# Two mixer stages of a hybrid backbone: priorities from the longest chain of data dependences instead of hand-written offsets

## The chip, the cores and the metric

One core of a Trainium2 chip runs the kernel. The metric is device time in microseconds (us), the median over runs of the whole program. The engines are PE (TensorE, matmul), DVE (VectorE), ACT (ScalarE), POOL (GpSimd) and SP (SyncE); SP, ACT and POOL also issue DMA transfers, each in the order of its own queue.

## What is computed

A backbone of two layers on 512 latent tokens (stream `l`) and 256 context tokens (stream `c`), D = 1024. Cut to what matters, each layer is

```
h        = rms_norm(x, g1) * (1 + scale1) + shift1       # modulated by the condition vector
u        = h @ W_in                                      # columns for four head groups of 256 channels
y        = concat(ssd(u), hyena(u), retention(u), s5(u)) # the mixers; latent tokens read the
                                                         # final context states of the recurrent ones
x        = x + gate1 * (y @ W_out)
f        = rms_norm(x, g2) * (1 + scale2) + shift2
x        = x + gate2 * ((silu(f @ W_g) * (f @ W_u)) @ W_d)
```

SSD is a chunked scan in both directions, Hyena a pair of long convolutions done as matrix products with cosine and sine tables (its filters come from a small MLP with sines), retention a chunked linear attention with rotations, S5 a diagonal complex state space model done in blocks. The second layer has no output for the context tokens.

## The kernel before

Everything is one program of some 15,000 instructions. A weight piece of 128 x 1024 floats is loaded into a staging tile `wst` (three buffers in a ring, issued on SP, L207), then split in two parts that TensorE takes at full precision together: `whi` by a copy on ACT (L155) and `wlo` by a subtraction on DVE (L134). The normed stream is split likewise (`ahl`/`alol` for the latent tokens, `ahc`/`aloc` for the context). A projection is three products a tile: `whi*ah`, `whi*al`, `wlo*ah` (`mm3`, called by `proj`, L233). All matmuls stand on line L126 in the profile, since one helper issues them; so the tiles' names tell them apart.

PSUM banks come from four rings: `mm` 3 banks, `xa` 2, `xb` 2, `md` 1. A "flow" of work takes banks from its own ring. `ps_mm` mostly holds products of the input projection, `ps_xb` those of Hyena and its filters, `ps_xa` those of SSD, retention and S5. The one bank `ps_md` holds in turn the modulation (`mod`, L334: 16 products `wst,csil` of a weight piece and the condition vector, ACT copies the row to `mrow`, PE turns it by a product with `const`, DVE adds the bias into `modv`) and the blocks of S5 (`s5k`, `KT`, `gt`).

What sets the order: each traced instruction carries a priority number, and a scheduler that walks through the program takes at each step, of the instructions whose inputs are there by its own estimate, the one with the lowest number. So each engine gets one fixed order, and at run time it waits in that order. Before, the numbers are counters that `body` (L1572) starts by hand:

- `at(p)` (L114) lets the instructions of a block count from p on; `flow(fl, p)` does so and sets the ring; `bulk()` (L240) adds 300000, so that the products of `proj` come after the mixers' own.
- `in_proj` (L1031) gives the q-th block of 256 columns the number PB + 4000q, and the modulation that is computed beside it PB + 2000q + 1000.
- The mixers start at `chunk(q)` = PB + 50000 + 2000q + 1000, with q chosen per mixer and layer: `chunk(2)` for Hyena of the context, `chunk((5, 0)[i])` for Hyena of the latent tokens, `chunk((-20, -5)[i])` for the output of S5, `chunk((4, 2)[i])` for SSD, and so on.
- In layer 0 the S5 tables (50000), the start (10000), the filters (35000 to 45000) and the S5 matrices (40000) have their own numbers.

The stages in order of time: start and norm of layer 0 (0 to about 90 us), layer 0's projection with filters, modulation, S5 blocks and mixers (to about 600 us), output projection and feed-forward, then layer 1's projection and mixers (about 1200 to 1585 us), and its feed-forward.

Of the kernel before, what the change touches and what calls it, by code (L numbers as in the profile page):

```python
# [9 lines left out]
F32 = mybir.dt.float32  # L10
# [8 lines left out]
L = 512  # L19
# [14 lines left out]
def halves(a):  # L34
    """A table as two float32 parts that float32r carries exactly."""
# [71 lines left out]
class Kern:  # L107
# [6 lines left out]
    @contextmanager  # L114
    def at(self, p):
        """Instructions in this block get priorities from p on."""
        tc = self.tc
        old, tc.cur_priority = tc.cur_priority, p
        try:
            yield  # L120
        finally:
            tc.cur_priority = old

# [37 lines left out]
    def pst(self):  # L161
        """A PSUM bank from the ring of the current flow of work."""
# [5 lines left out]
    def pst2(self, fl="mm+xb"):  # L168
        """As pst, from two rings in turn where no mixer runs."""
# [6 lines left out]
    def flow(self, fl, p=None):  # L176
        """Work that takes its banks and small tiles from rings of its own; p: its priority."""
# [10 lines left out]
    def rsq(self, v, n):  # L188
        """v: (128, n) tile, replaced by 1/sqrt(v)."""
# [13 lines left out]
    def piece(self, src, nk, ncol):  # L203
        """src: (128, nk * ncol) of a weight laid out by pieces."""
# [5 lines left out]
    def weights(self, srcs, nk=8):  # L210
        """Pieces of 128 columns as high and low parts."""
# [7 lines left out]
    def held(self, src):  # L219
        """Four tiles of rows of a weight with all its columns, src: (8, 128, 512)."""  # L220
# [20 lines left out]
    def bulk(self):  # L241
        """Products that fill the tensor engine come after the mixers' own."""
# [34 lines left out]
    def put_y(self, s, k, t, c0=0):  # L277
        """Keep tile k of the mixers' output: as operands of the output projection where these have room already."""
# [12 lines left out]
    def ytiles(self, s, p):  # L291
        """Tiles that are not written in the order of their making: each has its own place."""
# [41 lines left out]
    def mod(self, i, c0, c1):  # L334
        """Columns 256*c0 .. 256*c1 of the modulation of layer i."""
# [15 lines left out]
    def mod_vec(self, i, cols, both, p):  # L351
        """As mod for tiles of columns, with a column of the weights a row: products and sums on VectorE.
        The context stream has the tiles in both only."""
# [16 lines left out]
    def gains(self, i, part, s, gat):  # L370
        """(1 + scale) * g for a stream; part is 1 or 4."""
# [4 lines left out]
    def sq_acc(self, s, x, acc, first):  # L376
        """acc += x*x"""
# [7 lines left out]
    def rinv_rows(self, s, accs, scale, c0=0, c1=None):  # L385
        """Per-token 1/sqrt(scale * sum over channels + eps), broadcast to all partitions in PSUM."""
# [14 lines left out]
    def segs(self, s):  # L401
        """Ranges of tokens that are normed one after the other, so that products of one hide the norm of the next."""
# [1500 lines left out]
```

## Time and profile before

| | before |
|---|---|
| median of 3 runs | 1915.59 us (1913.96 to 1918.56) |
| span of the profiled execution | 1919.5 us |
| PE busy in it | 1790.1 us (93%) |
| DVE, ACT, POOL busy | 1257.5, 713.5, 207.3 us |
| moved by DMA | 280.87 MB, mean 146 GB/s |

For the profiled execution no time is given beside its span; the span lies 3.9 us above the median and 0.9 us above the longest of the runs shown. In the tables of the profile, "out<-in" names the tile written and the tiles read, "<-" behind a wait names what ended it, and PEclk is the TensorE clock that was granted as a share of full speed.

### The profile page before, as it was taken

To read this page: it belongs to the slowest core of one execution; us is meant where nothing else is said; L and a number is where in the kernel's file an instruction comes from. 1 tells how busy PE (TensorE), PEld (TensorE's weight loads), DVE (VectorE), ACT (ScalarE), POOL (GpSimd) and SP (SyncE) were. 2 spreads that over 40 slices of the span, in tenths; PEclk is the share of its full clock that TensorE was granted. 3 is DMA by queue.
4 is the path that set the end of the run, shared out by engine and by line. 5 is a ranking of instruction groups with operands and counts; after the bars stand their busy time and mean duration, and the time that the engine had idled before them with its cause. 6 is when DMAs were issued, how large, how long until landed. Compare 5 with 4: busy or idle time off the path is not lost.

```text
span 1919.5 us, 28992 instructions
## 1 busy us (share of the span) xinstructions
PE 1790.1 (93%) x10792; PEld 1526.3 (80%) x10792; DVE 1257.5 (66%) x2941; ACT 713.5 (37%) x1390; POOL 207.3 (11%) x273
## 2 busy tenths in 40 slices
PE   3789878898999999999999999989999999999997
PEld 2678767686789888888888989878866888888886
DVE  8788764778858899777665427678576843233336
ACT  4354234555227223212132115514673542222222
POOL 0201121123002000011223000121110000000000
PEclk9899979998899999999999999999997999999998
DMA  6656588765612335656635513565563322222331
GB/s 231 178 138 186 149 180 229 243 192 160 203 56 89 121 123 164 219 190 230 210 113 131 155 44 123 158 207 159 153 201 96 126 73 94 89 96 88 97 101 56
DMA packets 193089, 280.87 MB, mean 146 GB/s; under 512 B 51745, under 2 KB 127837, under 8 KB 192436
## 3 DMA queue, kind: packets, MB, share of 16 engines
q1 hardware_dynamic: 107188, 166.20, 28.5%
q10 hardware_dynamic: 55920, 64.72, 10.9%
q0 software_dynamic: 29840, 48.09, 8.9%
q8 instruction: 85, 1.39, 0.3%
q14 instruction: 56, 0.46, 0.1%
HBM read 235.00 MB, written 43.96 MB: 145 GB/s over the span
## 4 chain that ended last, share of the span: by engine, by line
PE 58%; DVE 11%; issue 8%; DMA 8%; ACT 3%; POOL 1%; ACTq 0%; SPq 0%; DVEq 0%; POOLq 0%
PE ps_mm L126 31%; PE ps_xb L126 20%; PE ps_xa L126 4%; DMA mvw<-in_wmt_dram 4%; PE ps_md L126 2%; DMA wst<-in_wi_dram 1%; ACT L155 1%; DVE mvo L364 1%; DVE wlo L134 1%; DVE gt L134 1%; DVE t L134 1%; DVE g L1499 1%; DVE cst L134 1%; DVE s5tmp L134 1%; ACT whi L155 1%
## 5 line engine op out<-in xcount | busy, mean ns | idle before, releaser
L155 ACT ACTIVATE whi<-wst 128x1024 fp32r<-128x1024 f32 (+3 forms) x226 | 198.9, 917 | 361.5 <-PE ps_mm L126 169.4
L134 DVE TENSOR_TENSOR wlo<-wst,whi 128x1024 fp32r<-128x1024 f32 (+3 forms) x226 | 233.9, 1058 | 83.5 <-ACT whi L155 81.2
L126 PE MATMUL ps_mm<-alol,whi 128*128 128x512 f32 (+1 forms) x688 | 262.7, 383 | 0.4 <-POOL alol L134 0.4
L126 PE MATMUL ps_mm<-ahl,wlo 128*128 128x512 f32 (+1 forms) x688 | 262.3, 382 | 0.0
L126 PE MATMUL ps_mm<-ahl,whi 128*128 128x512 f32 (+1 forms) x688 | 260.9, 383 | 0.3 <-ACT ahl L155 0.2
L126 PE MATMUL ps_mm<-h,whi 128*128 128x512 f32 (+1 forms) x592 | 168.8, 365 | 0.9 <-DVE h L134 0.7
L126 PE MATMUL ps_xb<-ahl,whi 128*128 128x512 f32 (+1 forms) x416 | 154.2, 373 | 3.8 <-ACT ahl L155 3.8
L126 PE MATMUL ps_xb<-ahl,wlo 128*128 128x512 f32 (+1 forms) x416 | 153.8, 370 | 0.0
L126 PE MATMUL ps_xb<-alol,whi 128*128 128x512 f32 (+1 forms) x416 | 153.5, 371 | 0.1
L134 DVE TENSOR_TENSOR sg<-sg,ps_mm 128x512 f32<-128x512 f32 (+1 forms) x70 | 39.9, 570 | 172.9 <-PE ps_mm L126 172.7
L126 PEld LDWEIGHTS ps_mm<-alol,whi 128*128 128x128 f32 x688 | 130.7, 190 | 26.4 <-issue 2.7
L126 PEld LDWEIGHTS ps_mm<-ahl,wlo 128*128 128x128 f32 x688 | 130.7, 190 | 24.5 <-issue 1.1
L126 PEld LDWEIGHTS ps_mm<-ahl,whi 128*128 128x128 f32 x688 | 130.2, 191 | 25.0 <-issue 1.6
L126 PE MATMUL ps_xb<-h,whi 128*128 128x256 f32 (+1 forms) x592 | 129.2, 310 | 0.1
L364 DVE SCALAR_TENSOR_TENSOR mvo<-mvw,crow 128x1024 f32<-128x1024 f32 x80 | 97.8, 1222 | 39.6 <-DMA mvw<-in_wmt_dram 38.7
L126 PE MATMUL ps_mm<-ahc,whi 128*128 128x256 f32 x368 | 107.4, 296 | 13.0 <-ACT whi L155 8.6
L126 PEld LDWEIGHTS ps_mm<-h,whi 128*128 128x128 f32 x592 | 103.7, 188 | 17.5 <-DVE h L134 1.2
L126 PE MATMUL ps_mm<-aloc,whi 128*128 128x256 f32 x368 | 108.2, 295 | 1.0 <-DVE aloc L134 1.0
L126 PE MATMUL ps_mm<-ahc,wlo 128*128 128x256 f32 x368 | 107.1, 293 | 2.0 <-DVE wlo L134 2.0
L126 PEld LDWEIGHTS ps_xb<-h,whi 128*128 128x128 f32 x592 | 98.9, 188 | 11.6 <-issue 1.1
L126 PE MATMUL ps_mm<-h,wlo 128*128 128x512 f32 (+1 forms) x296 | 107.9, 365 | 0.0
L155 ACT ACTIVATE h<-sg 128x512 fp32r<-128x512 f32 (+1 forms) x70 | 37.4, 534 | 161.7 <-DVE sg L134 161.6
(576 smaller groups left out, 4137.3 us busy)
## 6 DMA issues: line engine op xcount, KB each, us to landing
wst<-in_wu_dram SPq DMA_DIRECT2D x88, 512.0 KB
mvw<-in_wmt_dram POOLq DMA_DIRECT2D x56, 512.0 KB, 3.7
wst<-in_wi_dram SPq DMA_DIRECT2D x42, 512.0 KB
wst<-in_wm_dram SPq DMA_DIRECT2D x40, 512.0 KB
wst<-in_wd_dram SPq DMA_DIRECT2D x24, 384.0 KB
ftab<-in_c_ftL_dram POOLq DMA_DIRECT2D x32, 256.0 KB, 5.0
wst<-in_wd_dram SPq DMA_DIRECT2D x32, 256.0 KB
s5rot<-s5r SPq DMA_DIRECT2D x32, 192.0 KB
```

What stands on the lines that cost most here:

```text
L126: return self.nc.tensor.matmul(out, lhsT, rhs, start=start, stop=stop)
L134: return (eng or self.nc.vector).tensor_tensor(out, a, b, op=op)
L155: return self.nc.scalar.activation(out, in_, func, bias=bias, scale=scale)
L364: self.nc.vector.scalar_tensor_tensor(o, st, 1.0, crow[:, q], op0=ALU.mult, op1=ALU.mult, accum_out=mv[:, c, q:q + 1])
L1499: nc.vector.tensor_tensor_scan(o, dcy, x, 0.0, ALU.mult, ALU.add)
```

## The change

The program is traced twice. From the first trace, `priorities` computes for each instruction the length of the longest chain of data dependences from it to the end, with a length for each instruction from `length` (a table of costs by engine and size that the change writes down itself). Edges that only say that a buffer is free again are not followed. All matmuls into one PSUM tile share the rank of the first. In two ranges of the old numbers, 0 to 1500000 (all of layer 0 up to its output projection) and 2000000 to 2500000 (layer 1's projection and mixers), the instructions are sorted anew: first those that are not `bulk`, within each class those with the longer chain first, and numbered through. In layer 0 a product counts as `bulk` only from 1350000 on, so those that the start issues early do not. The second trace gives each instruction its new number. The norm of layer 1, both output projections and both feed-forwards keep the old numbers. What each instruction computes, its tiles and its engine stay; the rest of the diff takes out comments.

```diff
+class Ranked(tile.TileContext):
+    ranks = None
+    def instruction_hook(self, ins):
+        if not self.ranks:
+            return super().instruction_hook(ins)
+        keep = self.cur_priority
+        self.cur_priority = self.ranks.pop(0)
+        super().instruction_hook(ins)
+        self.cur_priority = keep + 1
+
+MIXED = ((0, 1500000), (2000000, 2500000))
...
+def length(i):
+    out = getattr(i.outs[0], "bass_ap", None) if i.outs else None
...
+    n = elements(out)
...
+    if kind == "InstDMACopy":
+        return 2500 + n * 128 // 50
+    if i.engine == mybir.EngineType.PE:
+        return max(112, 0.46 * n) if i.ins[0].dtype == F32R else 2 * max(112, 0.85 * n)
+    if i.engine == mybir.EngineType.Activation:
+        return 300 + 0.83 * n
+    if i.engine == mybir.EngineType.DVE:
+        return 200 + 1.04 * n
+    return 300 + 2.35 * n
+
+def priorities(nc, tc):
...
+    for q in reversed(range(len(ins))):
+        rank[q] += length(ins[q])
+        for name, info in nc.dependency_edges(ins[q].name):
+            if name in at and "DATA" in str(info):
+                rank[at[name]] = max(rank[at[name]], rank[q])
...
+            rank[q] = first.setdefault(key, rank[q])
+    out = [i.bass_priority for i in ins]
+    for lo, hi in MIXED:
+        inside = [q for q in range(len(ins)) if out[q] is not None and lo <= out[q] < hi]
+        big = [out[q] >= lo + (Kern.BULK + (1050000 if lo == 0 else 50000)) for q in inside]
+        order = sorted(zip(inside, big), key=lambda x: (x[1], -rank[x[0]], x[0]))
+        for n, (q, _) in enumerate(order):
+            out[q] = lo + n
+    return [0 if p is None else p for p in out]
...
-    with tile.TileContext(nc, schedule_with_timeline_sim=True) as tc:
-        Kern(tc, A, out).run()
-    return nc, arrays
...
+        tc = Ranked(nc, schedule_with_timeline_sim=True, name="kern")
+        if ranks is None:
+            tc.__enter__()
+            Kern(tc, A, out).run()
+            return priorities(nc, tc)
+        Ranked.ranks = ranks
+        with tc:
+            Kern(tc, A, out).run()
...
+    return trace(trace(None)), arrays
```

The new order differs from the old on every engine up to about 620 us of the trace and again from about 1200 to 1585 us; PE's instructions shift by up to some 150 places. Three places follow. The number behind a tile's name tells its buffers and uses apart.

**ACT in the start, before.** `nt` is the norm of one tile of the stream with the modulation applied (`modv0`, `gain`), `ahl` and `ahc` its rounded parts, `mrow_743` the copy of the fourth group of modulation that is needed.

```order
L155 ACTIVATE pb_685<-ps_xa_680 128x512
L1366 DMA s5r0_332<-cst_333 128x384
L155 ACTIVATE nt_709<-nt_709,modv0_86,gain_477 128x512
L155 ACTIVATE nt_714<-nt_714,modv0_86,gain_477 128x512
L155 ACTIVATE ahl_460<-nt_709 128x512
L155 ACTIVATE ahl_461<-nt_714 128x512
L1366 DMA s5r0_332<-cst_342 128x384
L155 ACTIVATE nt_698<-nt_698,modv0_86,gain_476 128x256
L155 ACTIVATE nt_703<-nt_703,modv0_86,gain_476 128x256
L155 ACTIVATE nt_720<-nt_720,modv0_86,gain_477 128x512
L155 ACTIVATE nt_725<-nt_725,modv0_86,gain_477 128x512
L155 ACTIVATE mrow_743<-ps_md_730 128x256
```

**The same place after the change.**

```order
L155 ACTIVATE pb_685<-ps_xa_680 128x512
L155 ACTIVATE mrow_743<-ps_md_730 128x256
L155 ACTIVATE nt_709<-nt_709,modv0_86,gain_477 128x512
L155 ACTIVATE nt_714<-nt_714,modv0_86,gain_477 128x512
L155 ACTIVATE ahl_460<-nt_709 128x512
L155 ACTIVATE nt_720<-nt_720,modv0_86,gain_477 128x512
L155 ACTIVATE nt_725<-nt_725,modv0_86,gain_477 128x512
L155 ACTIVATE nt_698<-nt_698,modv0_86,gain_476 128x256
L155 ACTIVATE nt_703<-nt_703,modv0_86,gain_476 128x256
L155 ACTIVATE ahl_461<-nt_714 128x512
```

`mrow_743` now stands ahead of six `nt` and two `ahl`, which it followed before, and right behind `pb_685`. On SP the start is put in another order too: the first modulation weights (`wst_479`) move from the 3rd issue to the 22nd, behind the 16 tiles of x (`xl`, `xc`), `rope`, `dtw` and two pieces of the input projection; from the 32nd issue on the next pieces follow as before.

**SP in the middle of layer 0, before.** `wst<-in_wm` are weights of the modulation, `wst<-in_wi` those of the input projection, `s5fu`, `s5fy`, `glw` the output of S5, `E` and `CE` belong to SSD of the context, `F0l` is the store of a Hyena filter's spectrum (`fo`). The first piece of the input projection that matters here, `wst_2970`, stands four issues above the first row, with `glw`, `s5fu` and `s5fy` behind it.

```order
L1537 DMA s5fy_4405<-s5y0_1633 128x8x32
L897 DMA E_4512<-acd0c_419 128x8x128
L964 DMA CE_4599<-acd0c_419 64x4x128 x2
L964 DMA CE_4611<-acd0c_419 64x4x128
L207 DMA wst_2974<-in_wi_dram 128x1024
L964 DMA CE_4611<-acd0c_419 64x4x128
L207 DMA wst_3099<-in_wm_dram 128x1024
L207 DMA wst_3105<-in_wm_dram 128x1024
L1535 DMA s5fu_4403<-s5u0_427 128x8x32
L598 DMA F0l_1279<-fo_1536 128x2x256
L598 DMA F0l_1279<-fo_1537 128x2x256
```

**The same place after the change.**

```order
L598 DMA F0l_1279<-fo_1536 128x2x256
L598 DMA F0l_1279<-fo_1537 128x2x256
L207 DMA wst_2957<-in_wm_dram 128x1024
L207 DMA wst_2970<-in_wi_dram 128x1024
L207 DMA wst_2974<-in_wi_dram 128x1024
L207 DMA wst_3099<-in_wm_dram 128x1024
L964 DMA CE_4599<-acd0c_419 64x4x128
L897 DMA E_4512<-acd0c_419 128x8x128
L964 DMA CE_4599<-acd0c_419 64x4x128
```

The two pieces of the input projection now follow one another, where `glw`, S5's loads and SSD's `E` and `CE` stood between them; but both, with the modulation's piece ahead of them, stand behind the two stores `F0l<-fo`, which before came five issues behind `wst_2974`.

**PE in layer 1, before.** `ps_xb<-cshi,qph` are products of Hyena of the latent tokens, `ps_md` a block of S5, `ps_mm<-ahc,whi` the input projection of the context.

```order
L126 MATMUL ps_xb_13912<-cshi_13770,qpl_13845 128x256
L126 MATMUL ps_md_14381<-s5U_14352,KT_14351 128x64
L126 MATMUL ps_xb_13939<-cshi_13770,qph_13844 128x256
L126 MATMUL ps_xb_13939<-cslo_13771,qph_13844 128x256
L126 MATMUL ps_xb_13939<-cshi_13770,qpl_13845 128x256
```

**The same place after the change.**

```order
L126 MATMUL ps_mm_13119<-aloc_12305,whi_13069 128x256
L126 MATMUL ps_mm_13119<-ahc_12297,wlo_13070 128x256
L126 MATMUL ps_xb_13939<-cshi_13770,qph_13844 128x256
L126 MATMUL ps_xb_13939<-cslo_13771,qph_13844 128x256
L126 MATMUL ps_xb_13939<-cshi_13770,qpl_13845 128x256
```

The products into `ps_xb_13939`, which followed those into `ps_xb_13912` with one product of S5 between them, now have 40 products of the input projection (16 into `ps_mm_13083`, 24 into `ps_mm_13119`, of which the last two are shown) between them and those into `ps_xb_13912`, and the product of S5 stands further ahead. Later products of this mixer, those into the last bank that DVE's `hx` reads, have more work of the projection ahead of them as well: the last of them stands 130 PE instructions later than before, and the first `hx` behind it 14 DVE instructions later. In layer 0 it is the other way round for this mixer: its products that ran at 352, 428 and 475 us of the trace (`zth`, `hin` and `qph` are what they read) come 32, 39 and 43 PE instructions earlier, and those of SSD at 362, 448 and 468 us 50, 27 and 20 later.

## Rows read from the trace of the kernel before

**Rows 1.** The page's part 1: busy us, share of the span, instructions.

```profile
PE 1790.1 (93%) x10792; PEld 1526.3 (80%) x10792; DVE 1257.5 (66%) x2941; ACT 713.5 (37%) x1390; POOL 207.3 (11%) x273
```

**Rows 2.** The page's part 4: the chain that ended last, by engine.

```profile
PE 58%; DVE 11%; issue 8%; DMA 8%; ACT 3%; POOL 1%; ACTq 0%; SPq 0%; DVEq 0%; POOLq 0%
```

**Rows 3.** Windows: length, busy us (instructions) by engine, PEclk, DMA share, GB/s.

```profile
0.00:48.00 48.00, 16.72 (x98) 9.63 (x99) 40.52 (x247) 22.29 (x49) 1.49 (x7) 1.00 0.64 231
48.00:96.00 48.00, 37.18 (x252) 30.64 (x251) 36.32 (x87) 17.06 (x33) 11.64 (x11) 0.86 0.62 178
96.00:288.00 192.00, 168.59 (x1069) 140.94 (x1067) 150.81 (x348) 79.80 (x164) 29.08 (x33) 0.92 0.66 163
288.00:384.00 96.00, 83.75 (x593) 68.32 (x593) 57.54 (x112) 49.46 (x100) 14.91 (x16) 0.93 0.80 236
384.00:576.00 192.00, 181.18 (x1246) 150.85 (x1245) 141.77 (x347) 76.51 (x175) 30.11 (x35) 0.93 0.49 153
1200.00:1392.00 192.00, 180.22 (x1144) 162.40 (x1143) 137.85 (x266) 93.20 (x161) 28.40 (x32) 0.96 0.58 169
1392.00:1584.00 192.00, 178.62 (x1074) 147.77 (x1073) 128.51 (x317) 97.61 (x212) 15.71 (x24) 0.91 0.39 124
6.00:58.00 52.00, 25.29 (x161) 16.89 (x162) 49.73 (x260) 24.46 (x55) 2.73 (x2) 1.00 0.59 214
```

**Rows 4.** PE's waits, 0 to 620 us: total us, times, longest us.

```profile
PE ps_xa L126 <- DVE rv L152: 9.1, 1, 9.1
PE ps_mm L126 <- ACT whi L155: 8.6, 1, 8.6
PE ps_md L126 <- DMA KT<-s5k: 9.7, 3, 5.6
PE ps_xb L126 <- ACT sE L155: 5.5, 1, 5.5
PE ps_md L126 <- DVE modv L134: 4.5, 3, 3.6
PE ps_mm L126 <- ACT ahc L155: 4.0, 2, 3.4
```

**Rows 5.** DVE's modv, 36 to 90 us: duration ns min/median/max, first and last start.

```profile
L134 DVE TENSOR_TENSOR modv<-ps_md,vec x6: 145/156/162, 44.5 to 84.8; 128x4 f32<-128x4 f32 x6
```

**Rows 6.** The timeline of SP, 262 to 297 us: start, us, what.

```profile
270.34 0.34 SPq L207 DMA_DIRECT2D wst<-in_wi_dram  x1
...
280.13 3.90 SPq L964 DMA_DIRECT2D CE<-acd0c  x3
284.13 0.55 SPq L207 DMA_DIRECT2D wst<-in_wi_dram  x1
...
288.38 2.68 SPq L598 DMA_DIRECT2D F0l<-fo  x2
```

**Rows 7.** The timeline of ACT, 283 to 296 us (idle before).

```profile
291.63 1.06 ACT L155 ACTIVATE whi<-wst 128x1024 fp32r<-128x1024 f32 x1 [2.07 <-DMA wst<-in_wi_dram]
```

**Rows 8.** Windows behind waits of PE, columns as in rows 3.

```profile
263.00:278.00 15.00, 12.64 (x70) 10.31 (x74) 8.55 (x16) 4.71 (x9) 4.12 (x6) 0.50 0.51 146
293.00:295.00 2.00, 2.00 (x6) 1.61 (x7) 2.00 (x4) 0.66 (x2) 0.00 (x0) 0.50 1.13 324
295.00:297.00 2.00, 2.00 (x9) 1.59 (x8) 0.81 (x2) 1.23 (x1) 0.00 (x0) 0.75 1.03 340
```

**Rows 9.** PE's waits, 1180 to 1600 us, columns as in rows 4.

```profile
PE ps_xa L126 <- DVE rrv L152: 4.5, 1, 4.5
PE ps_xa L126 <- ACT s5fy L155: 3.9, 1, 3.9
PE ps_xb L126 <- DVE vm L134: 3.4, 1, 3.4
```

**Rows 10.** DVE's hx, 1300 to 1425 us, columns as in rows 5.

```profile
L152 DVE SCALAR_TENSOR_TENSOR hx<-ps_xb,fr1l,hx x4: 474/474/477, 1357.9 to 1359.4; 128x256 f32<-128x256 f32 x4
```

**Rows 11.** A window behind hx, columns as in rows 3.

```profile
1358.00:1425.00 67.00, 63.08 (x350) 51.96 (x349) 35.80 (x89) 49.30 (x90) 4.59 (x11) 0.95 0.62 188
```

More of the change, by code (lines that the diff above doesn't have):

```diff
@@ L1880, in layout, with elements @@
     return A
+class Ranked(tile.TileContext):
[8 more added lines that the diff above has]
+MIXED = ((0, 1500000), (2000000, 2500000))
+def elements(ap):
+    return int(np.prod([n for _, n in list(ap.ap)[1:]], initial=1))
+def length(i):
+    out = getattr(i.outs[0], "bass_ap", None) if i.outs else None
+    if out is None:
+        return 0.0
+    n = elements(out)
+    kind = type(i).__name__
+    if kind == "InstDMACopy":
[7 more added lines that the diff above has]
+    return 300 + 2.35 * n
@@ new lines, in priorities @@
+def priorities(nc, tc):
+    ins = list(nc.cur_bb.bb.instructions)
+    tc._compute_data_deps()
+    at = {i.name: q for q, i in enumerate(ins)}
+    rank = [0.0] * len(ins)
+    for q in reversed(range(len(ins))):
[3 more added lines that the diff above has]
+                rank[at[name]] = max(rank[at[name]], rank[q])
+    first = {}
+    for q, i in enumerate(ins):
+        if i.engine == mybir.EngineType.PE and i.outs and hasattr(i.outs[0], "bass_ap"):
+            key = i.outs[0].bass_ap.tensor.name
+            rank[q] = first.setdefault(key, rank[q])
[7 more added lines that the diff above has]
+    return [0 if p is None else p for p in out]
@@ L1883, in build @@
 def build(inputs):
     import concourse.bacc as _bacc
-    nc = _bacc.Bacc("TRN2", target_bir_lowering=False, num_devices=1)
-    arrays, A = {}, {}
     given = {n: np.ascontiguousarray(a) for n, a in {**layout(inputs), **constants()}.items()}
-    for name, a in given.items():
-        arrays[f"in_{name}_dram"] = a
-        A[name] = nc.dram_tensor(f"in_{name}_dram", a.shape, mybir.dt.from_np(a.dtype), kind="ExternalInput").ap()
-    out = nc.dram_tensor("out_0_dram", (128, 8, L), F32, kind="ExternalOutput").ap()
@@ L1892, in build, with trace @@
-    with tile.TileContext(nc, schedule_with_timeline_sim=True) as tc:
-        Kern(tc, A, out).run()
-    return nc, arrays
+    arrays = {f"in_{name}_dram": a for name, a in given.items()}
+    def trace(ranks):
+        nc = _bacc.Bacc("TRN2", target_bir_lowering=False, num_devices=1)
+        A = {}
+        for name, a in given.items():
+            A[name] = nc.dram_tensor(f"in_{name}_dram", a.shape, mybir.dt.from_np(a.dtype), kind="ExternalInput").ap()
+        out = nc.dram_tensor("out_0_dram", (128, 8, L), F32, kind="ExternalOutput").ap()
+        tc = Ranked(nc, schedule_with_timeline_sim=True, name="kern")
[6 more added lines that the diff above has]
+            Kern(tc, A, out).run()
+            Ranked.ranks = None
+        return nc
```

## Prediction

> **What bounds the kernel now.** I read the page's first part, then the chain of waits, then windows by stage, then PE's waits inside them. PE is busy 1790.1 of 1919.5 us [rows 1] and holds 58% of the chain that ended last; DVE has 11%, DMA 8% [rows 2]. So the change can only win time in which PE stands still inside the two reordered ranges, or at a low clock. The windows give that time [rows 3]: 31.3 + 10.8 us idle in the first 96 us, 23.4 in 96 to 288, 12.3 in 288 to 384, 10.8 in 384 to 576, which is 88.6 us in layer 0; and 11.8 + 13.4 = 25.2 us in layer 1. Of these 113.8 us, the first 31.3 are mostly loads and DVE work that no order removes: from 6 to 58 us DVE is busy 49.7 of 52 us. To see in PE's waits [rows 4, 9]: no wait stands out; the longest are 9.1, 8.6, 5.6, 5.5 and 4.5 us, each ended by another chain. A reordering works on a dozen waits of 3 to 9 us, and a wait that it removes may come back elsewhere.
>
> The sum is made on differences and taken off the median, 1915.6 us; the profiled execution, with 1919.5 us, lies 0.2% above it, and its rows are used as they are. About 0.2% (3.8 us) is also what a measurement of this kernel can tell from no change.
>
> **The change, part by part.** No instruction is added or removed, so all cost is position: for each place I ask whether more or less work now stands ahead of it on its engine, and whether the wait there can close. Work is counted in products of 0.14 us in layer 0 (83.75 us for 593) and 0.16 us in layer 1 (180.22 for 1144) [rows 3].
>
> 1. *Start, 0 to 96 us.* The modulation goes round one bank and gives `modv` six times between 44.5 and 84.8 us [rows 5]; PE waits 4.5 us for it and 4.0 us for `ahc` behind it [rows 4]. The ACT order puts `mrow_743` ahead of eight activations that it followed. At most the 8.5 us of these two waits are won; at least nothing, because DVE has only 2.3 us free from 6 to 58 us [rows 3], and DVE makes both `modv` and the normed stream. Against it, the first modulation weights load behind all of x: 3 MB of x, 0.5 of `rope` and 1 of projection weights at the 231 GB/s of the first window take about 20 us, so the first modulation products start some 20 us later than if they led. The first `modv` is wanted at 44.5 us, so this is mostly covered; if 4 us of it show, the start is 4 us longer. Range -8.5 to +4; I take the middle of the gain, **-4**, since the ACT move hits the waits and DVE caps it.
>
> 2. *Weights and filters, about 230 to 300 us.* The longest wait of the middle is `whi`, 8.6 us [rows 4]. Its ACT copy began at 291.63, right when its piece landed [rows 7]; SP issued that piece at 284.13, though the piece before it went at 270.34, because loads for the output of S5 and three `CE` stood between, the latter 3.9 us long [rows 6]. Now the two pieces follow each other, and the wait could go whole: -8.6. But both stand behind the two `F0l` stores, which SP issued at 288.38 to 291.06 [rows 6]. If the filter is no earlier than before, the piece goes at 291 and not 284: +7. The stores and the filter's products are moved forward too, by some tens of PE instructions, so I take the half of the gain, **-4**. The clock speaks for a little more: behind this wait PE ran at 0.50 for 2 us and at 0.75 for 2 us [rows 8], 1.5 us of work lost, which go with the wait.
>
> 3. *300 to 576 us.* Here the order trades. Hyena's products at 352, 428 and 475 us come 32 to 43 places earlier, about 5 us each; PE reaches them sooner and waits there unless ACT and DVE are sooner as well. SSD's at 362, 448 and 468 us go 50, 27 and 20 places back and cover short waits. DVE is busy 199 of these 288 us [rows 3], so it can bring forward about a third of its part: of 15 us, 10 remain as new waits, and I put 7 of covered waits against them, **+3**. Ends: -10, if the 5.5 us for `sE` [rows 4] and a quarter of the other 17.6 idle us close; +10, if nothing is covered.
>
> 4. *Layer 1.* In the wait for `vm`, 3.4 us [rows 9], 40 products (40 x 0.16 = 6.3 us) are put ahead: it closes. The wait for `s5fy`, 3.9 us, should mostly close as well, as DVE comes earlier there; the one for `rrv`, 4.5 us, sits in a part of the order that hardly moves and stays. Of 7.3 us I take 2.3 back for a new wait in the one `md` bank: **-5**. Ends: -11.8, all three [rows 9]; +5, a new wait the size of the present longest.
>
> 5. *Feed-forwards, output projections, norm of layer 1.* Their order stays; 0. They start when the mixers end, so what is won or lost above passes through.
>
> Sum: -4 - 4 + 3 - 5 = -10, so **1905.6 us**.
>
> **A rule against it.** Rows 8 show that a stretch with several waits of 1 to 3 us is worse than it looks: from 263 to 278 us PE was busy 12.64 of 15 us and still had 0.50 of its clock all the way, the lower of its two levels (1.2 of 2.4 GHz). That is 6.3 us of work lost to the clock beside 2.4 idle. The Trainium skill, in "TensorE: Matmul & The Clock Gate", Part 1 "The HAM clock gate", says that the gate sets the rate by how busy the array has been recently, so that waits scattered through a stretch keep it low. The trace agrees with that by the 0.50 just named, and by this rule a change that breaks long waits into several short ones loses although the idle time is the same. The rival "clock" below is this, priced from the row.
>
> **The rivals.**
> - *DVE stands at `hx` (slower).* In layer 1 the last products ahead of Hyena's `hx` move 130 PE instructions back, 130 x 0.16 = 20.5 us, while `hx` moves only 14 DVE instructions, 14 x 137.85/266 = 7.3 us [rows 3]. DVE takes its work in order; it would stand at `hx` (before at 1357.9 [rows 10]) for up to 13 us, with S5, SSD and retention queued behind it. For it: from 1392 to 1584 PE already waits for DVE (`rrv`) [rows 9]. Against it: behind `hx`, from 1358 to 1425, DVE is busy only 35.8 of 67 us [rows 11], so 31 us are there to take up 13. It decides once these 31 us are not usable, because what stands in them waits for PE results that come later as well. Then layer 1 costs +13 in place of -5: 1915.6 - 4 - 4 + 3 + 13 = **1924 us**.
> - *SP's head (slower).* The stores of the filter are not ready, and all weights wait behind them: part 2 is +7, and the modulation and projection behind it put part 3 at its +10: -4 + 7 + 10 - 5 = +8, **1924 us**. For it: SP was at the stores only at 288.4 [rows 6]. Against: the products that feed them are moved forward.
> - *The clock.* Two more stretches like that at 263 us: -10 + 2 x 6.3 = +2.6, **1918 us**, no difference that shows.
> - *Nothing moves.* The waits are ended by chains (DVE in the start, S5's way through memory, one `md` bank) that the order doesn't shorten; each wait closed opens one next to it: **1915.6 us**.
> - *More than I count.* A chain-based order sees over the whole layer what hand offsets see by mixer. If half of the shown waits close beyond the start (9.7 + 8.6 + 5.5 + 4.5 + 3.9 + 3.4 = 35.6 [rows 4, 9], half is 18), with -4 in the start, the 6.3 at 263 us and 1.5 at 293 us given back by the clock [rows 8], it is -30: **1886 us**.
>
> **How the numbers follow.** Forecast 0.45 (its own range 1899 to 1911); more than I count 0.14; clock 0.06; nothing moves 0.09; `hx` 0.15; SP's head 0.11. So faster by over 0.2%: 0.59; within 0.2%: 0.15; slower: 0.26. The predicted time is the forecast's, 1905.6. The range, 1888 to 1927, takes in most of the larger gain and both slower cases with some 3 us of spread; about 2 in 10 lie outside, half on each side.
>
> **What would show it.** Part 1 right: the last `modv` starts before 82 us, and PE's waits for `modv` and `ahc` are together under 5 us; wrong: the first `modv` comes after 48 us. Part 2: no wait over 4 us for `whi`, and SP's issue of the second projection piece within 2 us behind the first; wrong: SP stands at `F0l` while PE waits for `whi`. Part 3: PE's idle time from 288 to 576 us between 20 and 30 us; new waits for `hin` or `qph`. Part 4: no wait for `vm`, idle time from 1200 to 1584 us about 20 us. The `hx` rival: DVE idle over 8 us directly ahead of `hx`, and PE waiting for DVE for over 20 us between 1392 and 1584. The clock: PEclk lower than now in the stage windows with no more idle time. More than I count: PE idle under 70 us in layer 0's range, and PEclk at 0.95 or more from 96 to 576 us.

## The result, and the profile after

The changed kernel takes 1942.97 us (median of 4 runs, 1934.81 to 1945.23), the kernel before 1916.73 us in the same comparison: ratio 1.0133, 95% interval 1.0109 to 1.0157. It is 26 us slower where 10 us less were forecast, and outside the range of 1888 to 1927 us. Its profiled execution took 1941.95 us with a span of 1940.2 us, 20.7 us over the span of before. The profiled execution of before, with 1919.5 us, is longer than any of its runs here, so the traces show some 21 of the 26 us.

The page's first part and the chain of waits [rows 1, 2]:

```profile
PE 1795.8 (93%) x10792; PEld 1527.5 (79%) x10792; DVE 1257.3 (65%) x2941; ACT 709.3 (37%) x1388; POOL 212.9 (11%) x273
...
PE 56%; issue 8%; DMA 6%; DVE 5%; ACT 1%; POOL 0%; SPq 0%; ACTq 0%; DVEq 0%; POOLq 0%
```

PE has hardly more busy time (1795.8 against 1790.1 us) in a longer span, so 15.0 of the 20.7 us are time in which PE stands still. Where, the windows tell; length, busy us (instructions) by engine, PEclk, DMA share, GB/s [rows 3]:

```profile
0.00:48.00 48.00, 12.28 (x73) 6.90 (x73) 38.81 (x236) 20.51 (x45) 0.76 (x6) 1.00 0.67 225
48.00:96.00 48.00, 40.05 (x261) 32.05 (x262) 40.56 (x97) 18.83 (x38) 12.85 (x12) 0.82 0.63 183
96.00:288.00 192.00, 168.90 (x1097) 140.95 (x1095) 151.92 (x354) 78.89 (x163) 30.12 (x31) 0.94 0.67 170
288.00:384.00 96.00, 87.28 (x614) 72.31 (x613) 52.78 (x110) 53.08 (x104) 16.39 (x18) 0.97 0.77 221
384.00:576.00 192.00, 167.50 (x1071) 136.40 (x1070) 134.49 (x311) 72.21 (x167) 31.03 (x32) 0.89 0.50 151
1200.00:1392.00 192.00, 183.41 (x1214) 166.18 (x1213) 144.47 (x288) 92.43 (x166) 31.31 (x35) 0.98 0.60 177
1392.00:1584.00 192.00, 174.28 (x1071) 144.37 (x1070) 130.40 (x329) 100.34 (x225) 16.35 (x24) 0.89 0.41 127
```

Up to 384 us nothing is lost: from 96 to 384 us PE stands still 31.8 us against 35.7 before, at a higher clock (0.94 and 0.97 against 0.92 and 0.93). From 384 to 576 us it stands still 24.5 us against 10.8, and the clock falls from 0.93 to 0.89. In layer 1 the idle time is 26.3 us against 25.2, in the same windows, although the changed kernel gets there 20 us later. PE's waits in layer 0, total us, times, longest [rows 4]:

```profile
PE ps_md L126 <- DMA wst<-in_wm_dram: 28.1, 4, 21.3
...
PE ps_xa L766 <- DMA rk<-drk0l: 7.5, 1, 7.5
PE ps_md L126 <- DVE modv L134: 4.3, 5, 2.3
...
PE ps_mm L126 <- ACT whi L155: 2.7, 3, 1.2
```

The wait for `whi` is gone (2.7 us in three). New are 7.5 us for `rk`, which is retention's load, and the long start: the first wait, 21.3 us for the first modulation weights, which now load behind all of x.

SP's queue in the middle of layer 0 [rows 6]:

```profile
268.85 1.21 SPq L598 DMA_DIRECT2D F0l<-fo  x2
270.57 0.34 SPq L207 DMA_DIRECT2D wst<-in_wm_dram  x1
271.01 4.74 SPq L207 DMA_DIRECT2D wst<-in_wi_dram  x2
...
288.82 0.55 SPq L1535 DMA_DIRECT2D s5fu<-s5u  x1
```

The stores `F0l` that stood at the head come at 268.85, not at 288.4, and the two weight pieces are issued at 271.0 and 275.4 instead of 270.34 and 284.13. The loads for the output of S5 (`s5fu`) pay for it: 288.82, before 271.5.

### The profile page after: what moved, and what is told of

It reads as the page before. It is cut to its first block, busy times and chain, and to the rows that moved or that the text cites. A ratio compares the mean times of both kernels' runs of the same rounds, so it can differ in the third digit from the quotient of the medians.

```text
span 1940.2 us, 28998 instructions
## 1 busy us (share of the span) xinstructions
PE 1795.8 (93%) x10792; PEld 1527.5 (79%) x10792; DVE 1257.3 (65%) x2941; ACT 709.3 (37%) x1388; POOL 212.9 (11%) x273
## 4 chain that ended last, share of the span: by engine, by line
PE 56%; issue 8%; DMA 6%; DVE 5%; ACT 1%; POOL 0%; SPq 0%; ACTq 0%; DVEq 0%; POOLq 0%
PE ps_mm L126 28%; PE ps_xb L126 21%; PE ps_xa L126 4%; DMA mvw<-in_wmt_dram 4%; PE ps_md L126 1%; DVE gt L134 0%; DMA wst<-in_wo_dram 0%; DVE xl L152 0%; DMA s5U<-s5u 0%; DVE wlo L134 0%; DVE mvo L364 0%; DMA s5ML<-s5m 0%; ACT L155 0%; DMA CE<-acd0l 0%; DMA E<-acd0l 0%
## 5 line engine op out<-in xcount | busy, mean ns | idle before, releaser
L126 PEld LDWEIGHTS ps_mm<-alol,whi 128*128 128x128 f32 x688 | 132.6, 193 | 25.2 <-issue 1.5
## 6 DMA issues: line engine op xcount, KB each, us to landing
wst<-in_wu_dram SPq DMA_DIRECT2D x88, 512.0 KB
mvw<-in_wmt_dram POOLq DMA_DIRECT2D x56, 512.0 KB, 3.6
wst<-in_wi_dram SPq DMA_DIRECT2D x42, 512.0 KB
wst<-in_wm_dram SPq DMA_DIRECT2D x40, 512.0 KB
```

What stands on the lines that cost most here:

```text
L126: return self.nc.tensor.matmul(out, lhsT, rhs, start=start, stop=stop)
```

## Where the time goes: the end of SSD

The mixers of layer 0 share space in SBUF: SSD of the latent tokens takes that of SSD of the context, retention of the latent tokens takes part of that of SSD of the latent tokens, and the operands of output projection A (`yhl`, `yhc`) another part. The chain can be followed by three instructions. Before: SSD's load (`sin<-dss0l`), its last store (`yd0l<-sin`), and the first product of output projection A (`yhl`), each with count, duration in ns, first and last start:

```profile
L864 ACTq DMA_DIRECT2D sin<-dss0l x1: 322/322/322, 395.2 to 395.2; - x1
L281 ACTq DMA_DIRECT2D yd0l<-sin x2: 326/326/326, 493.2 to 493.9; - x2
L126 PE MATMUL ps_mm<-yhl,whi x52: 275/284/792, 498.2 to 592.9; 128*128 128x256 f32 x32, 128*128 128x512 f32 x20
```

After:

```profile
L864 ACTq DMA_DIRECT2D sin<-dss0l x1: 341/341/341, 413.1 to 413.1; - x1
L281 ACTq DMA_DIRECT2D yd0l<-sin x2: 326/326/326, 505.3 to 505.9; - x2
L126 PE MATMUL ps_mm<-yhl,whi x35: 278/392/775, 512.2 to 600.0; 128*128 128x512 f32 x20, 128*128 128x256 f32 x15
```

The load comes 17.9 us later, the last store 12.0, output projection A 14.0. Why the load is late, DVE shows. SSD of the context ends with a chain of 13 small steps (`rv`, `rq`), a normalization. Before, DVE did it in one go, from 385.44 to 387.75 us:

```profile
385.44 0.15 DVE L149 TENSOR_SCALAR rv<-ps_xa 128x2 f32<-128x2 f32 x1
385.62 0.17 DVE L148 TENSOR_SCALAR rq_i<-rv 128x2 int32<-128x2 int32 x1
...
387.59 0.16 DVE L152 SCALAR_TENSOR_TENSOR rv<-rq_t,rv 128x2 f32<-128x2 f32 x1
390.66 0.69 DVE L134 TENSOR_TENSOR vp<-sE,ps_xb 128x512 f32<-128x512 f32 x1 [2.91 <-PE ps_xb L126]
...
391.86 0.87 DVE L152 SCALAR_TENSOR_TENSOR sin<-sin,vec,ps_xa 128x256 f32<-128x256 f32 x2
```

After, the same chain is spread out: between its steps stand steps of Hyena and of the projection, one of which waits 2.55 us for a load, and it ends at 402.5:

```profile
389.58 0.15 DVE L149 TENSOR_SCALAR rv<-ps_xa 128x2 f32<-128x2 f32 x1
389.70 0.69 DVE L134 TENSOR_TENSOR vt<-ps_mm,vmu 128x512 f32<-128x512 f32 x1
390.31 0.72 DVE L148 TENSOR_SCALAR rq_i<-rv 128x2 int32<-128x2 int32 x1
...
395.50 0.15 DVE L152 SCALAR_TENSOR_TENSOR rv<-rq_t,rv 128x2 f32<-128x2 f32 x1
...
398.80 0.69 DVE L134 TENSOR_TENSOR t<-vp,Ft 128x512 f32<-128x512 f32 x1 [2.55 <-DMA Ft<-F0l]
399.41 1.23 DVE L134 TENSOR_TENSOR rq_t<-rv 128x2 f32<-128x2 f32 x1
...
401.88 0.65 DVE L152 SCALAR_TENSOR_TENSOR rv<-rq_t,rv 128x2 f32<-128x2 f32 x1
```

The end of the chain is 14.8 us later than before: 4.1 us because it begins later, the rest because it is spread out. Only then can the context's result be stored (`yd0c<-sin`) and SSD of the latent tokens be loaded into its space; in the program the load waits for both stores. ACT's queue, before and after:

```profile
392.37 0.81 ACTq L281 DMA_DIRECT2D yd0c<-sin  x2
...
395.17 0.32 ACTq L864 DMA_DIRECT2D sin<-dss0l  x1
```

```profile
406.44 0.33 ACTq L281 DMA_DIRECT2D yd0c<-sin  x1
...
407.65 0.35 ACTq L281 DMA_DIRECT2D yd0c<-sin  x1
...
413.14 0.34 ACTq L864 DMA_DIRECT2D sin<-dss0l  x1
```

The load stands 5.5 us behind the second store, before 2.4: that is the other 3 of the 17.9 us. At the end of that mixer PE's timeline has (start, us, line, operation, and in brackets the idle time and what ended it):

```profile
511.86 0.66 PE L766 MATMUL ps_xa<-const,rk 128*128 128x128 f32 x2 [7.49 <-DMA rk<-drk0l]
512.17 0.78 PE L126 MATMUL ps_mm<-yhl,whi 128*128 128x512 f32 x1
```

PE stands 7.49 us, first for the end of SSD and then for `rk`, whose load stands right behind SSD's last stores in ACT's queue; output projection A comes right behind. One window, 400 to 520 us, holds most of the loss; before, and after:

```profile
400.00:520.00 120.00, 109.36 (x712) 87.31 (x711) 95.81 (x232) 61.49 (x140) 23.15 (x28) 0.89 0.57 180
```

```profile
400.00:520.00 120.00, 95.56 (x605) 76.38 (x606) 86.07 (x205) 55.44 (x128) 24.59 (x28) 0.83 0.57 168
```

13.8 us less busy time at a lower clock: 95.56 x 0.83 = 79.3 us of work at full clock against 109.36 x 0.89 = 97.3, that is 18 us.

## The experiments

The kernels differ in order and queues alone; none leaves work out. The ratio is to the kernel before as it was measured beside each run (medians of 1914.1 to 1916.7 us). "SSD's load", "SSD's store" and "projection A" are the starts of the three instructions above in the profiled execution.

| run | median us | ratio to before (95%) | SSD's load | SSD's store | projection A |
|---|---|---|---|---|---|
| before | 1916.73 | 1 | 395.2 | 493.9 | 498.2 |
| the change | 1942.97 | 1.0133 (1.0109 to 1.0157) | 413.1 | 505.9 | 512.2 |
| e1 layer 0 ranked | 1942.40 | 1.0145 (1.0123 to 1.0167) | 418.1 | 511.2 | 517.6 |
| e2 layer 1 ranked | 1914.17 | 0.9996 (0.9981 to 1.0012) | 391.9 | 490.6 | 494.9 |
| e3 space edges | 1950.37 | 1.0200 (1.0170 to 1.0229) | 402.7 | 514.2 | 520.2 |
| e4 whole tiles | 1969.50 | 1.0293 (1.0275 to 1.0311) | 404.7 | 515.9 | 522.2 |
| e5 SSD first | 1934.29 | 1.0100 (1.0080 to 1.0119) | 409.3 | 501.0 | 507.0 |
| e6 chain first | 1943.03 | 1.0148 (1.0130 to 1.0165) | 398.5 | 504.5 | 510.7 |
| e7 POOL queue | 1961.43 | 1.0247 (1.0223 to 1.0270) | 424.7 | 527.1 | 532.8 |
| e8 both | 1943.95 | 1.0143 (1.0113 to 1.0173) | 392.6 | 504.7 | 512.0 |
| e9 ACT freed | 1942.16 | 1.0154 (1.0135 to 1.0173) | 414.0 | 507.4 | 513.8 |
| e10 SSD first, ACT freed | 1937.44 | 1.0123 (1.0094 to 1.0152) | 408.5 | 502.5 | 509.1 |
| e11 front ranked | 1937.53 | 1.0132 (1.0107 to 1.0156) | 400.1 | 511.4 | 515.2 |
| e12 before, ACT freed | 1916.63 | 1.0012 (0.9997 to 1.0027) | 395.0 | 492.3 | 496.8 |
| e13 back ranked | 1954.46 | 1.0207 (1.0192 to 1.0223) | 418.7 | 521.9 | 528.1 |
| e14 random 0 to 7, layer 0 | 1935.30 | 1.0105 (1.0085 to 1.0125) | 406.0 | 508.5 | 512.3 |
| e15 random 0 to 2, layer 0 | 1929.84 | 1.0085 (1.0067 to 1.0103) | 400.3 | 505.0 | 508.8 |
| e16 random 0 to 7, layer 1 | 1904.69 | 0.9957 (0.9936 to 0.9979) | 392.6 | 490.0 | 494.3 |
| e17 random 0 to 7, second draw | 1942.40 | 1.0148 (1.0131 to 1.0165) | 403.4 | 513.4 | 519.8 |
| e18 as e16, second draw | 1911.95 | 0.9987 (0.9972 to 1.0003) | 391.9 | 488.9 | 493.2 |

**Which layer.** e1 and e2 each rank one of the two ranges.

```diff
-MIXED = ((0, 1500000), (2000000, 2500000))
+MIXED = ((0, 1500000),)                      # e1; e2: ((2000000, 2500000),)
```

> Only layer 0 is ranked; layer 1 keeps the hand-written numbers. PE's work done up to a given point, compared between the two traces, is 18 to 20 us later in the changed kernel at 600 us and 21 us later at 1600 us. If layer 0 carries the loss, this run is 16 to 22 us above the kernel before (1933 to 1939 us), with PE's new waits between 400 and 520 us still there. If layer 1 carried part of it, it would be less than 12 us above.

> Only layer 1 is ranked. By the same reading layer 1 costs 2 to 3 us: 1917 to 1921 us, within the measurement's uncertainty of the kernel before. By my prediction's part 4 (-5) it would be 1912 us. If the two ranges add up, the differences of this run and of the run with layer 0 alone sum to that of the changed kernel, 26 us.

Layer 0 carries the whole loss, and layer 1 nothing in either direction. e2 also goes through the second trace, with layer 0's numbers as they were, and loses nothing: taking the numbers from a list is not what costs.

**Space, or cut chains.** Two defects of the ranks are seen in the program itself. Chains end where a buffer must come free, since such edges are not followed: the last steps of SSD of the context have chains of 7 to 11 us by `length`, although SSD of the latent tokens and retention wait for them. And a chain is cut at every product that isn't the last to accumulate into its tile, because the reader of a tile depends by data on the last product alone. As all products into a tile share the rank of the first, the change does not rank by the longest chain there: of layer 0's 236 PSUM tiles that take several products, 108 are ranked under 0.5 us for this reason, as if hardly anything came behind them. e3 mends the first for two edges, e4 the second.

```diff
+        if type(ins[q]).__name__ == "InstDMACopy":                    # e3
+            src, dst = tname(ins[q].ins), tname(ins[q].outs)
+            for load, store, to in (("dss0l", "sin", "yd0c"), ("drk0l", "sin", "yd0l")):
+                if src == load:
+                    nexts[to] = max(nexts.get(to, 0.0), rank[q] + length(ins[q]))
+                if src == store and dst == to:
+                    rank[q] = max(rank[q], nexts[to])
...
+            key = ins[q].outs[0].bass_ap.tensor.name                   # e4, for products
+            rank[q] = max(rank[q], bank.get(key, 0.0))
+            bank[key] = rank[q]
```

> As the changed kernel, but two edges are added to the chains: SSD of the context (its last store) before the load of SSD of the latent tokens, and SSD of the latent tokens (its last store) before retention's load, since each waits for the space of the one before. Theory space (the ranks don't see that a buffer must come free, so the end of SSD of the context gets a low rank and is spread over other work on DVE): the load of SSD at 413 us comes at 393 to 400 us again, PE's wait of 7.5 us for rk goes or halves, and the time falls by 10 to 20 us against the changed kernel (1923 to 1933 us). Theory cut chains (ranks too short at accumulating products) and theory late weights (the last projection weights come 12 us later because the modulation holds the staging ring): less than 5 us better, 1938 to 1945 us.

> As the changed kernel, but a chain is no longer cut at the products that accumulate: all products into one PSUM tile get the longest rank among them before it is passed on to what feeds them. Theory cut chains: the order is then what the change says it is, and the time falls by 10 us or more (below 1933 us). Theory space: the end of SSD of the context stays among the shortest chains, so the wait for its space stays and the time stays within 6 us of the changed kernel (1937 to 1949 us).

e3 did at its place what it was to do (the load comes 10 us earlier than in the change), but the mixer that began earlier ended later, at 514.2 us, with Hyena late as well (its last store at 508.4 us, before 485.1), and the time rose. e4, in which accumulated products no longer cut the chains, is the slowest of all runs. So mending either defect by itself brings nothing back; both together were not run.

**SSD by hand inside the ranks, and its queue.** e5 puts both SSD mixers of layer 0 ahead of all else that is ranked, e6 also the output of S5; e7 issues SSD's loads `E` and `CE` on POOL, since in the ranked order SP had them behind two weight pieces; e8 is e6 and e7 together.

```diff
-        order = sorted(zip(inside, big), key=lambda x: (x[1], -rank[x[0]], x[0]))
+        order = sorted(zip(inside, big), key=lambda x: (x[1], not chain(x[0]), 0 if chain(x[0]) else -rank[x[0]], x[0]))
...
-            nc.sync.dma_start(e, bass.AP(
+            (nc.sync if i else nc.gpsimd).dma_start(e, bass.AP(
...
```

> As the changed kernel, but in layer 0 all instructions of both SSD mixers (context and latent tokens) come ahead of all other ranked ones, in the order of the program. In every ranked run so far out projection A starts 6 us behind SSD's last store, as before, and that store came 12 to 22 us late. Theory mixer chain (SSD late by its low ranks): the last store of SSD comes at 490 to 499 us (before 493.9, changed kernel 505.9) and the time is 1912 to 1925 us. Theory queue (SP issues SSD's E load behind two late weight pieces, in its order): E is still issued after 400 us, the store after 502 us, and the time stays above 1932 us.

> As e5_ssdfirst, and S5's output, which opens the chain S5 output, SSD context, SSD latent, retention latent and came 7 to 17 us late, also goes first. Theory mixer chain: S5's first load comes at 275 us or earlier again (changed kernel 288.8), SSD's last store before 497 us, the time 1908 to 1920 us. Theory queue: above 1930 us.

> As the changed kernel with its ranks, but in layer 0 the loads of SSD's E and CE are issued by POOL instead of SP, so that they don't stand behind weight pieces. Theory queue: E is loaded before 400 us and SSD's last store comes 6 to 12 us earlier than in the changed kernel (494 to 500 us), the time falls by 6 to 14 us (1929 to 1937 us). Theory mixer chain alone: SSD still waits for the end of SSD of the context at 407 us, and less than 4 us are gained (1939 us or more).

> Both together: the chain first and its E and CE loads on POOL. If each is a part of the loss, this is the fastest of the four: 1905 to 1917 us, SSD's last store before 494 us. If something else holds SSD (DVE, ACT), it is above 1925 us.

None of the four brought the gain. e5 is a third of a per cent better than the change, with intervals that overlap, and its SSD's store comes 4.9 us earlier. e6 starts SSD almost on time (398.5) and still ends it 10.6 us late: its chunk states (`Hn<-Hn,sS`) begin 3.2 us late and end 11.5 us late, at 481.9 us against 470.4. In time e5 and e6 came out where the theory "queue" had put them, but e7, which takes the loads off SP's queue, is much worse, and e8 is where "something else holds SSD" had put it. Each edit moves the order of all that follows, and what it wins at its place is lost behind it.

**Behind SSD's end.** e9 issues SSD's last stores and retention's loads on POOL, so that ACT's rounding of the operands of output projection A doesn't queue behind them; e10 does so on e5, e12 on the kernel before.

```diff
-            self.put_y(s, t, yz[t])
+            if i == 0 and s.name == "l":
+                nc.gpsimd.dma_start(s.yd[:, t, :], yz[t])
+            else:
+                self.put_y(s, t, yz[t])
...
-        nc.scalar.dma_start(kk, s.drk[:, 0:2])
+        (nc.gpsimd if i == 0 and lat else nc.scalar).dma_start(kk, s.drk[:, 0:2])
```

> As the changed kernel, but in layer 0 the two last stores of SSD (latent tokens) and the three loads of retention behind them are issued by POOL instead of ACT. On ACT the rounded tiles for output projection A (yhl) then stand no longer behind a store that waits for SSD's end, and in PE's order the first products of output projection A come ahead of retention's transposes of rk. Theory SSD's end (PE has nothing left to do until SSD of the latent tokens ends, and output projection A is queued behind it): output projection A starts at 503 to 506 us instead of 512.2, PE's wait of 7.5 us for rk goes, and the time falls by 6 to 10 us (1933 to 1937 us). If another chain holds PE there: less than 3 us.

> The same edit on e5_ssdfirst (1934 us). SSD's end: 1925 to 1929 us, as the two gains add (SSD 5 us earlier, output projection A 6 to 8 us closer behind it).

> The edit of e9_after_free on the kernel before. There, too, output projection A starts at 498.2 us behind SSD's store at 493.9 us, but PE waits until 496.3 us for retention of the context anyway: 1 to 5 us faster (1910 to 1914 us). If it is the same or slower, freeing ACT pays only where SSD is late.

No gain in any of them. In the order the products come ahead of retention's as meant, but ACT's timeline of e9 shows that the wait wasn't the queue:

```profile
503.28 0.72 ACT L155 ACTIVATE yhc<-yl 128x256 fp32r<-128x256 f32 x2 [6.15 <-DVE rq_t L134]
512.47 0.72 ACT L155 ACTIVATE yhc<-yl 128x256 fp32r<-128x256 f32 x2 [8.46 <-DMA yd0l<-sin]
513.09 2.17 ACT L155 ACTIVATE yhl<-yl 128x512 fp32r<-128x512 f32 x4
```

The third `yhc` waits 8.46 us, and not for the data it rounds, but until the store `yd0l<-sin` has read its tiles: in the program it waits for the two stores and for DVE, since the operands of output projection A lie in SSD's space too. So output projection A is held by SSD's end, whatever the queue. For retention queue and space aren't told apart: in every run its loads stand right behind these stores, on the same queue. In every run above projection A starts 3.8 to 7.3 us behind SSD's store.

**Which part of layer 0.** e11 ranks only the numbers below 1050000 (start, S5 tables, filters), e13 only those of the projection and the mixers.

```diff
-MIXED = ((0, 1500000), (2000000, 2500000))
+MIXED = ((0, 1050000),)                      # e11; e13: ((1050000, 1500000),)
```

> Ranked are only the numbers below 1050000, that is the start, the S5 tables and matrices and Hyena's filters of layer 0; the projection, the modulation beside it, the mixers and all of layer 1 keep the hand-written numbers. If the loss sits in the order of the mixers against each other, as SSD's end says, this is within 5 us of the kernel before (1910 to 1920 us) and SSD's last store comes at 491 to 497 us. If it were the front that makes all later: above 1925 us.

> The counterpart of e11_front: ranked are only the projection, the modulation beside it and the mixers of layer 0 (1050000 to 1500000); start, S5 tables and filters keep the hand-written numbers, and so does layer 1. Theory front: if the order of the front were the cause, this is within 5 us of the kernel before. Theory back: 15 to 25 us slower, and e11's loss is a second, separate one; then the two do not add, since both together cost 27. Theory tuned point: 10 to 30 us slower like every other order of layer 0, with SSD's last store after 500 us.

e11 refutes what I had by then. The mixers have their hand-written numbers in it, SSD begins at 400.1 us, and yet it ends at 511.4. Either part alone costs as much as the change or more, and the two don't add. e13 is slower than any of the ranges it was given. That fits no defect of a certain rank.

**Random changes.** The last four use no ranks: a random number is added to each hand-written one, in layer 0 (e14, e15, e17) or layer 1 (e16, e18).

```diff
+    rng = np.random.default_rng(1)           # e17, e18: 2
+    add = rng.integers(0, 8, len(out))       # e15: 3
+    out = [p if p is None or not 0 <= p < 1500000 else p + int(x) for p, x in zip(out, add)]   # e16, e18: 2000000 <= p < 2500000
...
```

> No ranks. The hand-written numbers of layer 0 stay, plus a random 0 to 7 on each instruction, so that neighbours change places, without a plan. Theory tuned point (the hand-written numbers give an order that was fitted to the measured one; any other interleaving ahead of 400 us makes the mixers' last stretch fit worse): 8 to 25 us slower, lost between 400 and 600 us. Theory ranks (it is the ranks that are bad): within 5 us of the kernel before.

> The same with a random 0 to 2. Theory tuned point: still 4 to 20 us slower, although each instruction moves by a place or two in the numbers. Theory ranks: within 3 us.

> A second draw of the random 0 to 7 on layer 0. If the loss belongs to leaving the fitted order and not to one unlucky draw: again 10 to 25 us slower (1925 to 1940 us), with SSD's last store after 500 us. If the first draws were unlucky: within 6 us of the kernel before.

> Random 0 to 7 on the numbers of layer 1's projection and mixers alone. Ranking layer 1 alone changed nothing (ratio 0.9996). If layer 1 has enough other work on PE to cover the mixers' chains, noise there changes nothing either: within 5 us. If it costs 8 us or more, the sensitivity is not special to layer 0.

> A second draw for layer 1, where the first one was 10 us faster (1904.7). If layer 1's hand-written order is simply not fitted, draws scatter around it on both sides: between 1900 and 1922 us. If it costs 10 us or more, the first draw was lucky and layer 1 is as sensitive as layer 0.

In layer 0 all three draws lose, 0.85% to 1.48%, and the change with its 1.33% lies among them. e15 leaves the order of layer 1 untouched on every engine; in e14 and e17 part of its end is reordered too. They lose at the same place. The window from 400 to 520 us of e14, e15 and e17, in this order (of before and after it is shown above):

```profile
400.00:520.00 120.00, 102.24 (x647) 81.31 (x646) 89.90 (x211) 57.04 (x130) 29.62 (x32) 0.82 0.52 163
```

```profile
400.00:520.00 120.00, 99.55 (x626) 79.36 (x624) 81.37 (x201) 53.97 (x128) 24.61 (x28) 0.84 0.54 167
```

```profile
400.00:520.00 120.00, 93.07 (x600) 73.62 (x599) 78.67 (x196) 52.86 (x123) 26.99 (x29) 0.83 0.53 157
```

That is 83.8, 83.6 and 77.2 us of work at full clock against 97.3 before and 79.3 in the change. SSD's store comes at 505.0 to 513.4 us. Over the whole table, the five kernels that keep layer 0's numbers (before, e2, e12, e16, e18) have this store at 488.9 to 493.9 us, and the fifteen with any other numbers there at 501.0 or later. In e15, where each number grew by 2 at most, PE's two longest waits in this window are the ones met above, the operands of projection A and SSD's load:

```profile
PE ps_mm L126 <- ACT yhl L155: 5.3, 1, 5.3
PE ps_xa L879 <- DMA sin<-dss0l: 3.7, 1, 3.7
```

That the draws lose without any rank shows that leaving this order is enough to lose about 1%. That the change loses for no other reason isn't shown: window and chain are the same, but its ranks have defects of their own.

In layer 1 the two draws give -0.43% and -0.13%, the second not clear of zero. e16, at 1904.69 us, beats both kernels, and is 10 us off where at most 5 were expected. Its layer 1 (the first window had 180.2 us busy at 0.96 before, the second 178.6 at 0.91 [rows 3]):

```profile
1200.00:1392.00 192.00, 184.48 (x1179) 164.14 (x1179) 143.65 (x277) 100.65 (x178) 29.20 (x33) 0.99 0.61 180
1392.00:1584.00 192.00, 177.42 (x1078) 147.24 (x1075) 123.99 (x300) 89.99 (x196) 14.34 (x22) 0.94 0.35 112
```

## Why the prediction was wrong, point by point

- **Part 1, the start (-4): no gain.** The last `modv` starts at 85.4 us, before at 84.8 [rows 5]:

```profile
L134 DVE TENSOR_TENSOR modv<-ps_md,vec x6: 149/154/163, 50.2 to 85.4; 128x4 f32<-128x4 f32 x6
```

  PE waits 4.3 us for `modv`, as before. I had named the mechanism against it, the modulation's weights behind all of x, and called it covered; the first `modv` of this stretch is 5.7 us late, over the 48 us that I had set as the mark, and what was won behind it, 5.1 us, only brought that back. The waits for `modv` and `ahc` together did fall under the 5 us that I had set, to 4.7, since `ahc` went from 4.0 to 0.4 us, while the wait for `ahl` grew from 1.2 to 3.8 us. And [rows 4] leave out the wait that is largest in total in the trace of before, 0 to 620 us:

```profile
PE ps_md L126 <- DMA wst<-in_wm_dram: 15.3, 5, 7.4
```

  PE waited for modulation weights already, so their later loads were not covered: now these waits are 28.1 us in four, the longest 21.3.
- **Part 2, weights and filters (-4): right, and too small.** The stores `F0l` were no hindrance, the wait for `whi` closed, and the clock came with it: from 96 to 288 us PEclk is 0.94 instead of 0.92, from 288 to 384 us 0.97 instead of 0.93, with 3.8 us less idle time in the two. With 168.90 x 0.94 + 87.28 x 0.97 against 168.59 x 0.92 + 83.75 x 0.93, PE does 243.4 us of work at full clock there against 233.0. The start lost 3.6 of these 10 (12.28 x 1.00 + 40.05 x 0.82 against 16.72 x 1.00 + 37.18 x 0.86), so PE is some 7 us ahead at 384 us. The 10 lie where they were forecast: from 230 to 300 us PE does 57.90 x 0.88 = 51.0 us of work against 53.21 x 0.77 = 41.0. The rival "SP's head" did not come true at this place.
- **Part 3, 300 to 576 us (+3): the step that failed.** It measured about +27 instead: the first product of the feed-forward (`h`) starts at 682.3 us, before at 662.4, 19.9 later, and 7 had been won by 384 us. 14.0 of the 19.9 are there at output projection A; of the other 6, 2.5 are two waits behind retention, and the rest isn't resolved. The motion was as forecast: Hyena's last store comes 5.7 us earlier (479.4 against 485.1), a new wait for `qph` of 3.8 us is there, and SSD is later. Its price was wrong: PE's idle time from 288 to 576 us is 33.2 us, not 20 to 30. I had counted places on PE, let DVE make up a third, and set 7 us of covered waits against the 10 that remained, all by the waits that the trace of before shows there, which are short. But that they are short belongs to the order of before. What ends this stretch is SSD, by way of space: loads that wait for space, operands of the next stage that lie in it. I followed data and engines and left space out, as the ranks do. And my upper end of +10 came from single waits, while here a lost microsecond counts until SSD ends, it seems because PE has little else by then: the 7 us that PE was ahead at 384 us are of no use to it.
- **Part 4, layer 1 (-5): nothing (e2, 0.9996).** The wait for `vm` closed as forecast, those for `s5fy` and `rrv` are gone as well, which was my end of -11.8, and others took their place [rows 9]:

```profile
PE ps_xa L126 <- DVE rq_t L134: 4.7, 1, 4.7
PE ps_xa L126 <- DVE vd L134: 3.5, 1, 3.5
PE ps_xb L631 <- DVE hin L152: 3.1, 1, 3.1
```

- **The rival `hx`** came true in its motion and not in its price: `hx` starts 35 us later [rows 10], some 20 of them layer 0's, so 15 by itself (13 were forecast). In e2, where layer 0 is as before, it starts at 1371.6 us, 13.7 later, and the run loses nothing; that DVE's idle time behind it took this up, as I had argued, fits but isn't shown by itself:

```profile
L152 DVE SCALAR_TENSOR_TENSOR hx<-ps_xb,fr1l,hx x4: 455/476/479, 1393.1 to 1398.5; 128x256 f32<-128x256 f32 x4
```

- **The rival "nothing moves", and the sign.** For a slower outcome I had two single mechanisms at 0.26 together. That the order of before may be better than its neighbours, so that almost any other is worse, was not among the rivals. It is the one that e14, e15 and e17 bear out for layer 0. The forecast took each visible wait as something to be won and gave no price to the waits that the present order avoids.
- **The clock.** From 400 to 520 us the granted clock fell from 0.89 to 0.83, with 13.8 us more idle time in the window. The Trainium skill, "TensorE: Matmul & The Clock Gate", Part 1 "The HAM clock gate", makes the rate follow how busy the array has been; the rows agree in both directions: 0.83 here, and 0.97 instead of 0.93 from 288 to 384 us, where PE's idle time fell from 12.3 to 8.7 us.

What stays open: which feature of the hand-written order brings SSD to its end by 494 us. Starting it on time isn't enough (e6, e8, e11, e15), and none of the ranked or random orders did it. That the numbers were fitted by trial is argued from their odd offsets and from this; it isn't shown.

## What to carry to other kernels

Before a new rule of order is judged, add small random numbers to the old priorities: if that alone costs 1%, as in layer 0 here, the old order is better than those around it, and a rule has to beat that and not the visible idle time. Ranks over data dependences leave out space; where stages hand a buffer space on, as SSD does to retention and to the output projection, the end of a stage is on the critical path though its data are wanted late. Where random changes cost nothing, as in layer 1, drawing a few orders and measuring them is a cheap gain: one of two draws won 0.43%.

## What the runs showed that I had not expected

Adding 0 to 2 to each priority, where blocks lie 2000 or 4000 apart, moved some 300 of the program's 9746 matmul instructions (the profile counts 10792), all in layer 0, and cost 0.85%. The scheduler decides by its own estimate of time what is ready, so one swap early on can change choices behind it. A queue that is freed (e7, POOL instead of SP) can cost 1.1 points more than the order that it was to mend (1.0247 against 1.0133).
